# A log-sum-exp on one core: VectorE's program aligned to a block of 256 instruction slots

## The chip, the cores and the metric

The kernel runs on one core of a Trainium2 chip. A core has five engines that run their own instruction streams side by side: TensorE (PE in the profile), VectorE (DVE), ScalarE (ACT), GpSimd (POOL) and SyncE (SP), and DMA engines that move data between the device memory and the core's on-chip memory. [...] The metric is device time in microseconds; the median of three runs before the change is 162.67 us (162.56 to 162.72).

## The reference

The input x is 32 x 512 x 1024 floats; the result is the logarithm of the sum of exponentials over the last axis, 16,384 numbers.

```python
def reference(x, axis):
    x_max = np.max(x, axis=axis, keepdims=True)
    return (x_max.squeeze(axis) + np.log(np.sum(np.exp(x - x_max), axis=axis))).astype(np.float32)
```

The values of x are normal random numbers, 67.1 MB in all.

## The kernel before, in words

The 16,384 rows lie 128 to a partition: partition p holds rows 128p to 128p + 127, each 1,024 floats long. The kernel leaves out the subtraction of the maximum at first: it computes log(sum(exp(x))) directly, tests afterwards whether every sum lies between LOW and HIGH, and only if one does not, goes through all data again with the maximum subtracted (the fallback, lines 292 to 326).

The list CHUNKS cuts the 128 rows of a partition into 17 chunks of 16 rows down to 1. SP issues their loads in order into a ring of 51 row places (`load`, lines 129 to 149); a load into places that were used before first waits until the engine that read them last has signalled. For each chunk ACT takes the exponential in place (line 201) in one or two parts, and VectorE sums the rows of each part (line 221, or by halves with the fused add and reduce at line 208). Some rows of the smaller chunks are summed by ACT itself, with the accumulating output of its exponential (lines 191 and 228). ACT also takes the logarithms in three pieces (line 156), and SP stores the result (line 241).

The end is a test. VectorE takes the largest and the smallest sum (lines 256 and 257), compares with the bounds (line 246), TensorE adds up the votes over the partitions with two small matmuls (lines 267 and 270), and VectorE puts the count into one number, the verdict (line 275). SP, VectorE and ACT each load the verdict into a register (line 280) and branch on it: with a full count they jump over the fallback (the condition at line 292, whose branch the profile shows at line 328). SP then clears the semaphores (line 329), waits until the store has landed, and takes its count back (lines 330 and 331).

Nothing is reordered by a scheduler: each engine runs its instructions in the order in which the kernel writes them. The instructions of all engines stand in a first block, which ends with a barrier of the five engines, and in the body that follows; only the first load is moved ahead of that barrier (lines 335 to 343). The waits of an instruction are for the most part carried by the instruction itself.

VectorE's stream has 2 instructions in the first block, 55 in the body up to and with the branch, and 10 in the fallback with a branch at its end. Around the program stand instructions of the runtime that no line of the kernel names.

## Time and profile before

| what | value |
|---|---|
| median of three runs | 162.67 us (162.56 to 162.72) |
| the profiled execution's own time | 162.66 us |
| its span, first to last instruction of the kernel | 160.9 us |
| busy: DVE, ACT | 121.9 us (76%), 115.1 us (71%) |
| read from device memory | 67.11 MB, 417 GB/s over the span |
| share of the loads' packets in the time of 16 DMA engines | 97.3% |

The span runs from the first load that SP issues to the last instruction of the kernel's program. What the runtime does ahead of it and behind it is not in the span; the profiled execution's time is 1.7 us longer than the span. In the views, "<-" in brackets names what ended the idle time before an instruction, an engine's name with a q (DVEq) is its sequencer, and L221 is line 221. The chain of work that ended last is followed back from the last instruction to what released it. The trace holds more than the page prints: every update of a semaphore with its time, and the packets that fetch instructions for the engines' sequencers.

### The profile page before, as it was taken

Reading aid. Unit: us, or ns where it says so; the run is one execution under the profiler, and the core shown is the slowest. Engines: PE = TensorE matmul, PEld = TensorE weight load, DVE = VectorE, ACT = ScalarE, POOL = GpSimd, SP = SyncE. Lnnn points to the kernel's source line nnn. Section 1 sums busy time; section 2 is a strip of 40 time slices with the busy share of each in tenths; the row PEclk is TensorE's granted clock in tenths of the full one; section 3 lists DMA queues with packets and bytes.
Section 4 is the critical chain, followed back from the end, with each engine's and each line's share of the span. In section 5 each row is a group of like instructions: output and inputs, shape, how many; then the busy total and the mean of one; then the engine's idle time right before and its main releaser. Section 6 shows DMA issues by size and latency. Waiting matters only on the chain.

```text
span 160.9 us, 147 instructions
## 1 busy us (share of the span) xinstructions
PE 0.2 (0%) x2; PEld 0.1 (0%) x2; DVE 121.9 (76%) x51; ACT 115.1 (71%) x40; POOL 0.4 (0%) x8
## 2 busy tenths in 40 slices
PE   0000000000000000000000000000000000000000
PEld 0000000000000000000000000000000000000000
DVE  0028000004999999999999599999999999999894
ACT  3170006995089960999429993999199999999995
POOL 1000000000000000000000000000000000000000
DMA  7999799979989989989979999999999999999990
GB/s 269 497 489 489 321 412 521 440 342 521 424 358 521 424 358 521 424 358 521 424 326 456 456 456 440 424 424 424 413 412 412 474 420 403 433 428 425 402 405 31
DMA packets 2592, 67.18 MB, mean 417 GB/s; under 512 B 288, under 2 KB 416, under 8 KB 928
## 3 DMA queue, kind: packets, MB, share of 16 engines
q1 hardware_dynamic: 2592, 67.18, 97.3%
HBM read 67.11 MB, written 0.07 MB: 417 GB/s over the span
## 4 chain that ended last, share of the span: by engine, by line
DMA 49%; DVE 30%; ACT 20%; issue 0%; PE 0%
DMA ring<-in_x_dram 49%; DVE sums L221 29%; ACT ring L201 17%; ACT ring L228 3%; ACT ring L191 1%; ACT res L156 0%; DVE above L246 0%; PE votes L267 0%; DVE verdict L275 0%; PE votes L270 0%
## 5 line engine op out<-in xcount | busy, mean ns | idle before, releaser
L221 DVE TENSOR_REDUCE sums<-ring 128x8 f32<-128x8192 f32 (+5 forms) x14 | 111.2, 7994 | 36.8 <-ACT ring L201 36.8
L201 ACT ACTIVATE ring<-ring 128x8192 f32<-128x8192 f32 (+6 forms) x18 | 104.4, 5836 | 43.5 <-DMA ring<-in_x_dram 43.4
L208 DVE CUSTOM_DVE_ANT_0 ring<-ring 128x512 f32<-128x512 f32 x16 | 9.9, 688 | 0.0
L228 ACT ACTIVATE ring<-ring 128x1024 f32<-128x1024 f32 x8 | 8.2, 1042 | 0.0
L172 ACT ACT_TABLE_LOAD x1 | 1.3, 1283 | 0.8 <-PEq L360 0.8
L228 ACT ACTIVATION_READ_ACCUMULATOR ring<-ring 128x1 f32 x8 | 1.4, 176 | 0.0
L208 DVE DVE_READ_ACCUMULATOR2_ANT sums<- 128x1 f32 x16 | 1.3, 84 | 0.0
L191 ACT ACTIVATE ring<-ring 128x1024 f32<-128x1024 f32 x1 | 1.0, 1039 | 0.0
L246 DVE TENSOR_TENSOR above<-late,bounds 128x8 bf16<-128x8 f32 x1 | 0.2, 167 | 0.7 <-ACT res L156 0.7
L156 ACT ACTIVATE res<-sums 128x81 f32<-128x81 f32 (+1 forms) x2 | 0.5, 248 | 0.0
L275 DVE TENSOR_REDUCE verdict<-votes 1x1 int32<-1x6 f32 x1 | 0.2, 153 | 0.3 <-PE votes L270 0.3
L256 DVE TENSOR_REDUCE ends<-sums 128x1 f32<-128x124 f32 x1 | 0.3, 282 | 0.1
L267 PE MATMUL votes<-above,weights 128*1 128x6 bf16 x1 | 0.2, 166 | 159.6 <-DVE above L246 159.6
L257 DVE TENSOR_REDUCE ends<-sums 128x1 f32<-128x124 f32 x1 | 0.3, 270 | 0.0
L246 DVE TENSOR_TENSOR above<-ends,bounds 128x4 bf16<-128x4 f32 x1 | 0.2, 163 | 0.1
L156 ACT ACTIVATE res<-late 128x4 f32<-128x4 f32 x1 | 0.2, 173 | 0.0
L270 PE MATMUL votes<-above,weights 128*1 128x6 bf16 x1 | 0.2, 165 | 0.0
L267 PEld LDWEIGHTS votes<-above,weights 128*1 128x1 bf16 x1 | 0.1, 79 | 159.6 <-DVE above L246 159.6
L191 ACT ACTIVATION_READ_ACCUMULATOR ring<-ring 128x1 f32 x1 | 0.2, 155 | 0.0
L173 POOL MEMSET bounds<- 128x6 f32 x1 | 0.1, 104 | 0.4 <-POOLq L360 0.4
L174 POOL MEMSET bounds<- 128x6 f32 x1 | 0.1, 102 | 0.0
L176 POOL MEMSET weights<- 128x1 bf16 x1 | 0.1, 102 | 0.0
(6 smaller groups left out, 0.6 us busy)
## 6 DMA issues: line engine op xcount, KB each, us to landing
ring<-in_x_dram SPq DMA_DIRECT2D x1, 7680.0 KB, 24.7
ring<-in_x_dram SPq DMA_DIRECT2D x1, 7168.0 KB, 28.7
ring<-in_x_dram SPq DMA_DIRECT2D x1, 6656.0 KB, 35.8
ring<-in_x_dram SPq DMA_DIRECT2D x1, 4608.0 KB, 20.2
ring<-in_x_dram SPq DMA_DIRECT2D x2, 2048.0 KB, 16.0
ring<-in_x_dram SPq DMA_DIRECT2D x1, 3584.0 KB, 28.3
ring<-in_x_dram SPq DMA_DIRECT2D x1, 2560.0 KB, 27.3
ring<-in_x_dram SPq DMA_DIRECT2D x4, 512.0 KB, 27.0
```

What stands on the lines that cost most here:

```text
L156: nc.scalar.activation(out=res[:, lo:hi], in_=src, func=Ln, bias=bias).then_inc(act_done, 1)
L172: nc.scalar.preload_act_table_set("natural_log_exp_and_others")
L191: nc.scalar.activation(out=ring[:, s, lo:hi], in_=ring[:, s, lo:hi], func=Exp, accum_out=late[:, LATE - 1 + k : LATE + k],).then_inc(act_d ...
L201: nc.scalar.activation(out=ring[:, s + lo : s + hi], in_=ring[:, s + lo : s + hi], func=Exp).then_inc(act_done, 1)
L208: nc.vector.tensor_tensor_reduce(out=ring[:, s + j, : D // 2], in0=ring[:, s + j, : D // 2], in1=ring[:, s + j, D // 2 :], scale=1.0, scal ...
L221: nc.vector.reduce_sum(out=sums[:, row + lo : row + hi], in_=ring[:, s + lo : s + hi], axis=AX).then_inc(dve_done, 1)
L228: nc.scalar.activation(out=ring[:, s + j], in_=ring[:, s + j], func=Exp, accum_out=total(row + j),).then_inc(act_done, 1)
L246: nc.vector.tensor_tensor(out=above[:, :, lo:hi], in0=values.unsqueeze(1).to_broadcast([P, 2, hi - lo]), in1=bounds[:, :, lo:hi], op=Alu.i ...
L256: nc.vector.reduce_max(out=ends[:, :1], in_=sums[:, :late_row], axis=AX).then_inc(dve_done, 1)
L257: nc.vector.tensor_reduce(out=ends[:, 1:], in_=sums[:, :late_row], axis=AX, op=Alu.min).then_inc(dve_done, 1)
L267: nc.tensor.matmul(votes[:1, :K], lhsT=weights[:, :1], rhs=above[:, 0], start=True, stop=False)
L270: nc.tensor.matmul(votes[:1, :K], lhsT=weights[:, 1:], rhs=above[:, 1], start=False, stop=True).then_inc(counted, 1)
```

## The change

One statement is added ahead of the loop over the chunks. It is a directive on VectorE's stream to the loader: the next instruction of that engine is to stand at a slot number divisible by 256 (a slot holds one instruction of 64 bytes). The loader drops the directive and fills in as many slots as are missing. With `max_nops=0` none of the padding is executed: its first slot becomes a branch to the aligned instruction. The next instruction of VectorE is the first reduction (line 221, in the changed kernel line 224). The other engines' streams and the order of VectorE's instructions stay as they are; every line number behind the statement grows by three.

```diff
     nc.gpsimd.memset(weights[:, :1], 1.0)
     nc.gpsimd.memset(weights[:, 1:], -TOO_MANY).then_inc(pool_done, 1)
+
+
+    nc.vector.addr_align(256, max_nops=0)
 
     logged = 0
     done_before = [(0, 0)]
```

## The prediction

> **What bounds the kernel now.** I read the head of the page first, then the chain of work that ended last, then who waited for whom, then the start and the end of the timeline, and last the records that lie outside the span.

> ```profile
> span 160.9 us, 147 instructions
> ...
> PE 0.2 (0%) x2; PEld 0.1 (0%) x2; DVE 121.9 (76%) x51; ACT 115.1 (71%) x40; POOL 0.4 (0%) x8
> ...
> DMA 49%; DVE 30%; ACT 20%; issue 0%; PE 0%
> DMA ring<-in_x_dram 49%; DVE sums L221 29%; ACT ring L201 17%; ACT ring L228 3%; ACT ring L191 1%; ACT res L156 0%; DVE above L246 0%; PE votes L267 0%; DVE verdict L275 0%; PE votes L270 0%
> ```

> Half of the chain is the load of x, nearly all the rest is work on data that has landed, and "issue", time that nothing in the profile explains, is 0%. So inside the span no engine stands still for want of an instruction. The waits of VectorE (group, us in total, times, longest) say the same:

> ```profile
> DVE sums L221 <- ACT ring L201: 36.8, 4, 23.1
> DVE above L246 <- ACT res L156: 0.7, 1, 0.7
> DVE verdict L275 <- PE votes L270: 0.3, 1, 0.3
> ```

> All of its idle time is ended by another engine's data. The start of the timeline shows how early VectorE's program begins and how late it is needed:

> ```profile
> 0.88 0.10 POOL L176 MEMSET weights<- 128x1 bf16 x1
> 7.32 3.62 ACT L201 ACTIVATE ring<-ring 128x4096 f32<-128x4096 f32 x1 [5.26 <-DMA ring<-in_x_dram]
> 10.97 4.42 DVE L221 TENSOR_REDUCE sums<-ring 128x4 f32<-128x4096 f32 x1 [10.97 <-ACT ring L201]
> 25.50 13.00 ACT L201 ACTIVATE ring<-ring 128x15360 f32<-128x15360 f32 x1 [14.56 <-DMA ring<-in_x_dram]
> ```

> VectorE passes the opening barrier at 0.73 us (its semaphore wait runs from 0.711 for 0.021) and has nothing to do before 10.97. At the end, the branch over the fallback (L328) on the three engines that take it:

> ```profile
> L328 SPq COMPARE_BRANCH  x1: 45/45/45, 160.5 to 160.5; - x1
> L328 ACTq COMPARE_BRANCH  x1: 45/45/45, 160.5 to 160.5; - x1
> L328 DVEq COMPARE_BRANCH  x1: 67/67/67, 160.6 to 160.6; - x1
> ```

> The profiled execution took 162.66 us, its span is 160.94, so 1.72 us lie around the span; the median of the runs shown is 162.67, the same time. No view of the page reaches those 1.72 us, but the trace also holds semaphore updates and the packets of the instruction queue there. Times from the span's start, in us:

> ```
> last instruction: ACT branch ends 160.576, DVE branch ends 160.698, SP's last semaphore step ends 160.938
> semaphore 2, which no line of the kernel names: 159.954 | 160.775 160.814 161.351 161.374 | 161.472 161.510 161.544 161.591
> semaphore clears by block of numbers: 161.487 (207-255), 161.601 (156-206), 161.643 (54-104), 161.657 (105-155), 161.811 to 162.158 (7-53)
> semaphore 2 again: 162.422 162.456 162.494 162.539 162.562 | 162.659 162.698 162.732 162.779
> instruction queue: one packet of 8192 bytes at 161.819, 0.455 long
> ```

> Semaphore 2 steps five times up and four times back, a barrier of the five engines after the program. Where nobody is late, the up-steps are 34, 38, 45 and 23 ns apart (the second barrier). In the first one the fourth step is 0.537 us behind the third instead of 0.045, and all that follows waits for it. That is the place where the change can act.

> The first step (159.954) is TensorE's, the only engine then finished that had worked so late (its last result is signalled at 159.796, 0.158 before). Of ACT, SP and VectorE the first to end is ACT: 160.576, and the second step is 0.199 later. SP can't be at 160.775 or 160.814, it still runs its program. VectorE can hardly be, its branch has ended only 0.077 and 0.116 before. I take the fourth for VectorE and the fifth for SP, whose clears (the narrowest spacing, as in its own clear at L329) come first after the turn. Then VectorE needs 0.653 us from its branch to the barrier, ACT 0.199.

> **What could keep VectorE 0.45 us.** Its program is the longest: 2 instructions before the barrier's end, 55 up to the branch, 10 in the fallback and a closing branch; ACT has 44 in all, SP 38, PE and POOL 16 together. The only instruction packet near the end starts at 161.819, 1.12 us after VectorE's branch. The result's store shows the same lag: issued at 159.363, first packets about 160.21 to 160.53, landed after 1.5 us. So my reading is that VectorE's taken branch passes from one fetch block to the next, that this costs about 0.4 to 0.45 us, and that the packet is the refill which it triggers. It isn't a block fetched on demand: that would not have been there before 162.27 (161.819 + 0.455), and the fourth step comes at 161.351.

> **The change part by part.** One directive ahead of VectorE's first reduction. It removes no instruction, moves none between queues, and adds no wait and no DMA of the kernel; SP's and POOL's queues hold what they held.

> 1. Padding and its jump. VectorE executes one branch more at 0.73 us. The nearest row is L328 on DVE, 0.067 us. It lies in the idle time that ends at 10.97 with ACT's result (10.2 us of cover), so 0. If that cover were gone it would cost itself, 0.07.

> 2. Reaching the new block. It may need a fetch at 0.73 us, amid the loads. Lower bound 0 (the block is there). From the end of the trace a fetch takes 1.12 + 0.455 = 1.6 us in quiet queues. Among loads each packet of 61,440 bytes holds an engine for 2.3 us, so behind two of them it is about 1.6 + 4.6 = 6.2 us, landing at 6.9. The worst row is queueing behind everything, as the loads do (issue to landing, us):

> ```profile
> ring<-in_x_dram SPq DMA_DIRECT2D x1, 7168.0 KB, 28.7
> ring<-in_x_dram SPq DMA_DIRECT2D x1, 6656.0 KB, 35.8
> ...
> out_dram<-res SPq DMA_DIRECT2D x1, 64.0 KB, 1.5
> ```

> The first reduction takes 4.42 us and the second starts at 38.53, when ACT's second exp is done; so VectorE's start may slip to 34.1 us before anything later moves. Taken: 6.9 < 10.97, so 0. The bytes (16 KB at 417 GB/s) are 0.04 us of the loads, and I take 0 for them, too.

> 3. The crossing at the end goes. The 66 slots of body and fallback now start at slot 0 of a block of 256, and the code behind them has some 190 slots left. VectorE then would reach the barrier at 160.698 + 0.199 (ACT's row; with its slower branch, 67 to 45 ns, up to 0.30), so at 160.90 to 161.00 instead of 161.351.

> 4. What is late next: SP. It waits for the store's landing (last update 160.904) and ends at 160.938. From its last step to the barrier nothing is recorded; TensorE needed 0.158 and ACT 0.199 with a taken branch. By these, SP steps at 161.10 to 161.14 instead of 161.374, a gain of 0.24 to 0.28; if SP needs only 0.06, the gain is 0.37, and if it was as late as VectorE by itself, 0. I take 0.27, by the row that has no branch in it, as SP has none either, and some more haste of SP's sequencer (its semaphore waits last 17 ns, TensorE's 51). The rest of the tail hangs on this step and moves with it.

> Sum: 162.66 - 0.27 + 0 + 0 = 162.39 for the profiled execution, 162.40 against the median.

> [...]

> **The rivals.**

> A, the forecast: 162.40, by itself 162.28 to 162.52.

> B, nothing: the 0.45 us aren't the block's. VectorE's code behind the branch may be longer than ACT's, the fourth engine may be another, or SP may be the late one itself. For it: the fetch packet carries no engine's name, and VectorE is slower in the two rows next to it as well (its load of the verdict takes 545 ns, SP's 462). Against it: the packet's time. Time 162.67.

> C, more: the refill at 161.819 also holds the second barrier, whose first step (162.422) comes 0.148 after the packet's end at 162.274. Without it the step would follow the last clear (162.158) by TensorE's 0.158, at 162.316, 0.106 earlier; with A's 0.27 that is 0.38, 162.29. Against it: the block of clears that ends last isn't VectorE's by the order above.

> D, the other side: the jump at the end finds the code behind it not loaded. That takes the 1.6 us of item 2 from 160.698, and 0.2 to the barrier: 162.48 instead of 161.351, so 1.1 us more, 163.8. It decides only if the runtime's closing code has more than some 190 instructions, or if the aligned block's successor is never fetched ahead; one refill seen at the end speaks against both. A late fetch at the start would be its kin: past 34.1 us each us costs one, and with the 35.8 us row it would be 2.5, 165.1.

> **How the numbers follow.** A 0.59, B 0.21, C 0.08, D and its kin 0.12. A measurement of this kernel tells about 0.2%, 0.33 us, from no change, so the bound lies at 162.34. A's price is an estimate with about 0.07 us to either side, and some 18 of its 59 parts lie below that bound: faster 0.18 + 0.08 = 0.26; same 0.41 + 0.21 = 0.62; slower 0.12. The range takes in A, B and C with the spread of the runs (0.08 to each side): 162.22 to 162.78; D is left out.

> **What would show it.** Item 3 is right if the fourth step of semaphore 2 comes within about 0.3 us of VectorE's branch and the instruction packet at the end is gone; item 4 if SP's step comes 0.1 to 0.2 us after its last one; items 1 and 2 if an instruction packet shows in the first microseconds and the first reduction still starts at 10.97. Inside the span nothing should differ by more than 0.1 us. The prediction fails if VectorE is as late as before (B), or if the packet at the end stays while its step comes later (D).

## The result

The changed kernel takes 163.77 us (median of 6 runs, 163.68 to 163.83) against 162.66 us before (6 runs, 162.55 to 162.72): ratio 1.0070, 95% interval 1.0057 to 1.0083. It is 1.1 us slower, where the prediction said 162.40 and gave slower 0.12.

The profiled execution took 163.80 us. Its span is 162.435 us, 1.497 more than before; around the span lie 1.365 us, 0.357 less than before (1.722). So the end became cheaper, by somewhat more than the 0.27 forecast, and something inside the span, where the prediction saw nothing, cost four times as much. The head of the page and its list of DMA queues (packets, megabytes, share of 16 engines):

```profile
span 162.4 us, 148 instructions
...
q1 hardware_dynamic: 2592, 67.18, 96.4%
q14 instruction: 2, 0.02, 0.0%
```

Before, the list had q1 alone. Now two packets of the instruction queue fall inside the span. The chain that ended last, in order of time (start, us, what), of the kernel before:

```profile
0.78 24.69 DMA ring<-in_x_dram
...
25.50 13.01 ACT ring L201
...
38.53 16.16 DVE sums L221
...
54.71 28.93 DMA ring<-in_x_dram
...
122.02 24.68 DMA ring<-in_x_dram
```

and of the changed kernel:

```profile
0.78 26.25 DMA ring<-in_x_dram
...
27.05 13.01 ACT ring L204
...
40.09 16.16 DVE sums L224
...
56.27 28.83 DMA ring<-in_x_dram
...
123.48 24.72 DMA ring<-in_x_dram
```

The whole loss is in the first piece: 26.25 instead of 24.69, 1.56 us. Every later piece has its old length within 0.1 us and only starts later. Nor does VectorE wait for its own instructions; its three waits end as before, on other engines' data:

```profile
DVE sums L224 <- ACT ring L204: 38.2, 4, 24.1
DVE above L249 <- ACT res L156: 0.7, 1, 0.7
DVE verdict L278 <- PE votes L273: 0.3, 1, 0.3
```

The timeline shows both first loads late, and VectorE following them:

```profile
7.93 3.62 ACT L204 ACTIVATE ring<-ring 128x4096 f32<-128x4096 f32 x1 [5.88 <-DMA ring<-in_x_dram]
11.58 4.42 DVE L224 TENSOR_REDUCE sums<-ring 128x4 f32<-128x4096 f32 x1 [11.58 <-ACT ring L204]
27.05 13.00 ACT L204 ACTIVATE ring<-ring 128x15360 f32<-128x15360 f32 x1 [15.50 <-DMA ring<-in_x_dram]
```

ACT's first exponential starts 0.61 us later than before, its second 1.56. The reason stands in the records of single packets. The trace names no DMA engine, but in the first 26 us of the changed kernel's profile the packets sort into 16 rows by start and end, each packet starting within 0.012 us of the end of the one ahead of it. I take a row for an engine. Both instruction packets are in one row (start, us, length, bytes):

```
row with the instruction packets                 another row of the same profile
 4.172  0.611  16384                              4.589  0.611  16384
 4.779  0.309   8192  instruction                 5.197  0.611  16384
 5.085  1.147  16384                              5.804  0.611  16384
 ...                                              ...
 9.727  2.267  61440                              9.287  2.267  61440
11.991  0.321   8192  instruction                11.551  2.267  61440
12.300  2.929  61440                             13.814  2.267  61440
 ...                                              ...
ends the second load at 26.566                   the other 15 end it at 24.527 to 25.184
```

Each instruction packet takes 0.31 to 0.32 us itself, and the load packet behind it takes 0.54 and 0.66 us longer than its kind. That is 1.82 us on one engine of sixteen. Without them the row would have ended at about 24.75, among the others. The rest of the load waits for it: 26.566 against 25.174 for the latest row before. The load's semaphore shows the same without any sorting into rows. It takes 16 steps; fifteen are there by 25.551, the last comes at 27.031 (before: fifteen by 25.386, the last at 25.473), and ACT starts 0.02 us behind it. So 1.39 of the 1.56 us is the late row; the other 0.17 lies between the row's end and the last step (0.465, before 0.299), and no run shows why.

The end, by the same kind of records as in the prediction:

```
                                  before     changed
DVE's branch ends                160.698     162.195
fourth step of semaphore 2       161.351     162.440   (0.653, now 0.245 behind the branch)
SP's last step ends              160.938     162.435
fifth step                       161.374     162.570   (0.436, now 0.135 behind SP)
last clear to second barrier       0.264       0.264
instruction packet at the end    161.819        none
```

### The profile page after: what moved, and what is told of

It reads as the page before. It is cut to its first block, busy times and chain, and to the rows that moved or that the text cites. A ratio compares the mean times of both kernels' runs of the same rounds, so it can differ in the third digit from the quotient of the medians.

```text
span 162.4 us, 148 instructions
## 1 busy us (share of the span) xinstructions
PE 0.2 (0%) x2; PEld 0.1 (0%) x2; DVE 121.9 (75%) x51; ACT 115.1 (71%) x40; POOL 0.4 (0%) x8
## 4 chain that ended last, share of the span: by engine, by line
DMA 49%; DVE 29%; ACT 20%; issue 0%; PE 0%
DMA ring<-in_x_dram 49%; DVE sums L224 29%; ACT ring L204 17%; ACT ring L231 2%; ACT ring L194 1%; ACT res L156 0%; DVE above L249 0%; PE votes L270 0%; DVE verdict L278 0%; PE votes L273 0%
## 5 line engine op out<-in xcount | busy, mean ns | idle before, releaser
L156 ACT ACTIVATE res<-sums 128x81 f32<-128x81 f32 (+1 forms) x2 | 0.5, 250 | 0.0
L270 PE MATMUL votes<-above,weights 128*1 128x6 bf16 x1 | 0.2, 166 | 161.1 <-DVE above L249 161.1
L156 ACT ACTIVATE res<-late 128x4 f32<-128x4 f32 x1 | 0.2, 173 | 0.0
L270 PEld LDWEIGHTS votes<-above,weights 128*1 128x1 bf16 x1 | 0.1, 79 | 161.1 <-DVE above L249 161.1
## 6 DMA issues: line engine op xcount, KB each, us to landing
ring<-in_x_dram SPq DMA_DIRECT2D x1, 7168.0 KB, 28.6
ring<-in_x_dram SPq DMA_DIRECT2D x1, 6656.0 KB, 35.7
```

Of the source, the lines that this page charges most:

```text
L156: nc.scalar.activation(out=res[:, lo:hi], in_=src, func=Ln, bias=bias).then_inc(act_done, 1)
L270: nc.tensor.matmul(votes[:1, :K], lhsT=weights[:, :1], rhs=above[:, 0], start=True, stop=False)
```

## The experiments

The theory (T): two instruction packets among the loads make one DMA engine late, and a load lands with its slowest engine. The rivals: the loss belongs to VectorE or to aligned code as such, to the bytes, or to the first two loads alone. For the end, the theory C: VectorE's late step is the branch passing a block's end.

On the chips of these runs the kernel before spread wider than above (162.5 to 163.3 us), so each is read by its ratio to the runs of the kernel before beside it. Where one profile is set against the one profile of the kernel before, 0.1 to 0.2 us are of that spread: in the seven profiles whose first loads no instruction packet touches and no copy joins (late_align, mid_align, late128 and the four with empty instructions), the second exponential starts at 25.57 to 25.69, against 25.495 before. The diffs of mid_align, steal and the runs with empty instructions are against the kernel before, that of late128 against late_align, the others against the changed kernel.

**late_align: the directive ahead of the last compare instead.**

```diff
-    nc.vector.addr_align(256, max_nops=0)      # ahead of the loop over the chunks
...
     compare(0, 2, ends)
+    nc.vector.addr_align(256, max_nops=0)
     nc.vector.wait_ge(act_done, acts)
     compare(2, K, late[:, :n_late])
```

> The directive stands ahead of VectorE's last compare instead of ahead of its first reduction. Theory T (the two instruction packets of 8192 bytes rob one DMA engine in the middle of the loads, and a load lands with its slowest engine): the refill now comes after 158 us, when all loads have landed, so the span stays 160.9 (within 0.1), and the barrier after the program is freed of the crossing as in the changed kernel (the fifth step of semaphore 2 0.14 us behind SP's last step instead of 0.44): 162.36 (162.3 to 162.45). VectorE's jump lies in the 0.73 us in which it waits for ACT's last result. Rival L (aligned code as such, or the longer program, slows loads or engines, wherever the refill falls): span 162.4, time 163.8. Rival J (the jump costs VectorE more than its idle 0.73 us): the last compare starts later than 159.37 and the time lies between 162.5 and 163.5.

Measured: 164.61 us, ratio 1.0103 (1.0084 to 1.0122). VectorE's waits:

```profile
DVE sums L221 <- ACT ring L201: 37.0, 4, 23.1
DVE above L246 <- issue: 2.9, 1, 2.9
```

"issue": nothing in the profile ended this wait. The jump starts at 158.776 and the next instruction at 161.766, 2.99 us later, although ACT's result was there at about 159.6. The first instruction packet runs from 159.776 to 160.269, the second comes at 162.636, after VectorE has gone on. The loads were on time (second exponential at 25.613, before 25.495), so L falls and T holds for them. The forecast of the time missed: VectorE is late, as J says, and by more than J's range (to 163.5). What VectorE waited for no record names. That the code at the place the jump leads to was not there is my estimate, from the packet of 8192 bytes that runs within the wait; late128 below makes the jump shorter. The barrier was freed here too: its fourth step comes 0.245 behind VectorE's branch.

**pool_only: GpSimd aligned instead of VectorE.**

```diff
     nc.gpsimd.memset(weights[:, 1:], -TOO_MANY).then_inc(pool_done, 1)
+    nc.gpsimd.addr_align(256, max_nops=0)
-    nc.vector.addr_align(256, max_nops=0)
```

> VectorE's stream is as before; GpSimd, which has nothing to do after 0.98 us, is aligned behind its last memset instead. Theory T: GpSimd's refill robs a DMA engine in the same way: packets of the instruction queue in the first 15 us, first load 0.3 to 0.6 us later, second load 1.0 to 1.6 us later, end as before: 163.7 to 164.3. Rival V (the loss belongs to VectorE, its stream or its jump): no change, 162.66. No refill, if GpSimd's stream ends in the block that it jumps to and none is fetched: 162.66 as well, but then without instruction packets among the loads, which would decide nothing.

Measured: 163.74 us, ratio 1.0057 (1.0035 to 1.0080). Its packets, and the first piece of its chain:

```profile
q14 instruction: 2, 0.02, 0.0%
```

```profile
0.79 25.62 DMA ring<-in_x_dram
...
26.43 13.01 ACT ring L202
```

The packets come at 4.797 and 11.689, in one row that ends the second load at 25.945 against 25.326 for the latest of the others; the second exponential is 0.94 us late, a little under the 1.0 to 1.6 expected. VectorE's stream is unchanged, and the end is as late as before (0.651 from its branch to the fourth step). So the loss isn't VectorE's: rival V falls. The stretch behind the packets is smaller than for VectorE's, 0.22 and 0.35 us.

**both_start: VectorE and GpSimd aligned.**

```diff
+    nc.gpsimd.addr_align(256, max_nops=0)
...
     nc.vector.addr_align(256, max_nops=0)
```

> The changed kernel with GpSimd aligned as well. Theory T, where a load lands with its slowest DMA engine: if the two engines' refills go through different DMA engines, both are late side by side and the cost is the larger one: 163.6 to 164.0; if through the same, it adds up: 165.0 to 165.4. Rival S (what counts is the total of bytes or packets taken from the loads): adds up in either case, about 164.9 to 165.4, with the packets on two DMA engines.

Measured: 163.73 us, ratio 1.0054 (1.0035 to 1.0074). Four packets, in two rows, which end the second load at 25.97 and 26.73; the others end by 25.27. The load's semaphore has fourteen steps by 25.620 and the last two at 26.422 and 27.194. Twice the packets cost no more than VectorE's two alone (1.0070): here the slowest engine counts, not the sum. Rival S falls.

**mid_align: the directive ahead of the third chunk.**

```diff
     for i, (r, n_dve, parts, by_halves) in enumerate(CHUNKS):
+        if i == 2:
+            nc.vector.addr_align(256, max_nops=0)
```

> The directive stands ahead of VectorE's third chunk, so that the jump comes at about 38.6 us and the refill between 39 and 50 us, among packets of 65,536 bytes. Theory T: 16 DMA engines stay busy to the end, so what one engine loses there stays lost: the load that lands at 83.6 before comes 0.9 to 2 us late, and the end with it; with the barrier's 0.30 us back, 163.2 to 164.4. Rival F (only the first two loads are sensitive, later ones have slack): span 160.9, time 162.36.

Measured: 163.82 us, ratio 1.0063 (1.0044 to 1.0083). Packets at 44.070 and 49.747. In its chain the first load piece has its old length, the second is longer (28.93 before):

```profile
0.79 24.77 DMA ring<-in_x_dram
...
54.80 30.27 DMA ring<-in_x_dram
```

The loss, 1.34 us, moved with the packets. Rival F falls.

**slots_run: the padding executed.**

```diff
-    nc.vector.addr_align(256, max_nops=0)
+    nc.vector.addr_align(256, max_nops=255)
```

> The changed kernel, but the padding is executed as empty instructions instead of being jumped over, in VectorE's idle first 10 us. Theory T: what counts are the instruction packets among the loads. If straight-line code has its next block loaded ahead, one packet at most falls among the first loads instead of two: second load 0.4 to 1.0 us late, time 162.8 to 163.4 with the end's 0.30 back. If the two packets remain, 163.8 as with the jump.

**nops20: 20 empty instructions instead of a directive.**

```diff
+    for _ in range(20):
+        nc.vector.engine_nop()
```

> No directive. VectorE executes 20 empty instructions ahead of its first reduction, in its idle first 10 us, so all of its later code moves by 20 slots and is not jumped to. Theory T with crossing C (VectorE's late step in the barrier before the change is the branch at the end passing a block's end): the block's end now falls 10 to 20 instructions ahead of that branch, about 148 to 152 us, and is passed in straight line. No instruction packet among the first loads; one at about 149 to 153, when the chain of waits runs through ACT and no longer through the loads; span 160.9, the fifth step of semaphore 2 0.14 us behind SP's last step instead of 0.44, time 0.30 below before: ratio 0.998. Rival J (passing a block's end stalls VectorE for about 3 us in straight line too, as the jump did in the late run): a gap without a cause between two of the half sums, and since the last of them is due at 157.8, 0.5 to 2.5 us above before. Rival N (the late step is not the block's): the same as before, ratio 1.000.

Measured: 162.88 us, ratio 1.0008 (0.9997 to 1.0020): no gain. Yet the barrier is freed (fifth step 0.136 behind SP). The one packet comes at 147.681, the load packet behind it takes 1.12 us instead of 0.46, and the last load packet ends at 158.081 instead of 157.524. Neither J nor N: the loads still mattered there, which the expectation denied. Half of it was wrong: T holds longer than I thought.

**steal: two foreign packets of about the same size.**

```diff
+    for k in range(2):
+        nc.scalar.dma_start(out=scratch[k : k + 1],
+            in_=bass.AP(tensor=x.tensor, offset=x.offset, ap=[[2039, 1], [1, 2039]])).then_inc(extra, 16)
...
+    nc.sync.wait_ge(extra, 32)
     nc.sync.wait_ge(passed, 2)
```

> VectorE as before. ACT's queue copies 8156 bytes of x within device memory, twice, as one packet each, in its first 2 us; nothing reads the copy. Theory T (a foreign packet on one DMA engine makes that engine late, and the loads wait for it): packets of that size among the first load's, each followed by a longer load packet as in the changed kernel, the engine 0.7 to 1.8 us behind the others, the second load later by 0.5 to 1.5 us and the end by as much: 163.1 to 164.2. Rival I (the loss is peculiar to instruction fetches): no more than the bytes, 0.04 us: 162.7.

Measured: 163.08 us, ratio 1.0026 (1.0011 to 1.0040). The list of queues:

```profile
q1 hardware_dynamic: 2592, 67.18, 97.1%
q10 hardware_dynamic: 4, 0.02, 0.0%
```

The two packets of 8156 bytes stand at 4.830 and 6.355 in one row, 0.308 us each, and the load packets behind them have their usual 0.611. So the engine loses 0.62 us, not 0.7 to 1.8, and ends at 25.390, hardly behind the next (25.342); the second exponential starts at 25.766, at most 0.2 us behind that of the untouched runs above. Of the 0.36 us between the medians (163.08, before 162.72), 0.24 lie around the span (1.95 us, before 1.71), where no load is; the spans have medians of 161.1 and 161.0. So T's range of 0.5 to 1.5 us for the loads is missed, and the result is nearer to I: the bytes of two foreign packets cost the loads about 0.1 us. The stretch of the packet behind is, in these runs, peculiar to instruction packets, and it makes up 1.20 of the 1.82 us of the changed kernel's late row; why it comes is not shown.

**late128, start128: 128 slots instead of 256.**

```diff
-    nc.vector.addr_align(256, max_nops=0)
+    nc.vector.addr_align(128, max_nops=0)
```

> As the late run, with 128 slots in place of 256. From the run with executed padding: the gap of 0.46 us after the 61st of 189 empty instructions says that blocks are 128 slots long and that VectorE's first reduction stands at slot 67 of 256, so the last compare, 51 instructions on, stands at slot 118. Padding to 128 is 10 slots, into the block that follows. Theory T with crossing C: passing into the block that follows costs 0.41 us, here inside the 0.73 us in which VectorE waits for ACT; one refill packet about 159.5 to 160.5, after the loads; no 3 us gap; barrier freed: span 160.9, time 0.30 below before, ratio 0.998. Rival J2 (every jump to a block's first slot fetches it anew): last compare 2 to 2.4 us late as in the late run, 164.5.

> The changed kernel with 128 slots in place of 256: the padding is 61 slots and the jump leads into the block that follows. Theory T: one packet instead of two among the loads, at 2 to 9 us, 0.31 long and the load packet behind it 0.5 to 0.7 longer; the engine 0.85 to 1.0 late, the second load 0.4 to 0.9; with the end's 0.30 back 162.8 to 163.3. If the number of packets doesn't matter, or two come again, 163.8.

Measured for late128: 162.55 us, ratio 0.9984 (0.9971 to 0.9997), a little faster than before. The last compare starts when ACT's result is there (159.616, after a wait of 0.73 us as before), the crossing is hidden, one packet comes at 159.909. J2 falls: the 2.99 us of the late run came with the leap from slot 118 to 256, and the jump from 118 to 128 has none of them.

Measured for start128: 162.73 us, ratio 0.9998 (0.9987 to 1.0009), below the 162.8 to 163.3 expected and the same as before. One packet at 4.775; its row ends the second load at 25.600, and the second exponential starts at 26.095, 0.41 to 0.53 behind the untouched runs. The spans of all runs put the loss at 0.3 us (median 161.4, before 161.1), and about as much comes back around the span (1.34, before 1.71): the two cancel.

**nops10, nops14, nops15: where the refill falls.** The edit is that of nops20 with another count.

> 10 empty instructions ahead of VectorE's first reduction, no directive: the block's end falls just ahead of the last compare, in straight line. Theory T with crossing C: as with the directive of 128 slots at that place, crossing hidden in the wait for ACT, refill packet after the loads (158.5 to 160.5), not at 147.7 as with 20 empty instructions: time 0.25 to 0.30 below before, ratio 0.998. If the refill comes earlier than VectorE's place suggests, before 157, a load is late again and the ratio is 1.000 to 1.003.

Measured: 162.50 us, ratio 0.9982 (0.9969 to 0.9995), packet at 159.968. But SP's last step comes 1.87 us behind the store's issue, before 1.56 (in late128 1.71). The refill lies just ahead of the store's packets (from 160.311), and of the 16 steps of the store's semaphore one alone is late: fifteen by 161.014, the last at 161.314 (before 160.877 and 160.904). So here, too, one engine's share lands last.

> 14 empty instructions: the block's end falls just behind VectorE's bare semaphore wait ahead of the largest sum (157.83 in the kernel before), so the refill is asked for then and its packet should come at 159.0 to 159.5, between the last load (157.5) and the store's packets (160.2), instead of 159.9 to 160.0 as with 10, where the store landed 0.15 to 0.30 us later than without. VectorE's 0.41 us lie in its 0.73 us of slack. If so: store's issue to SP's last step 1.56 us as before, barrier freed, ratio 0.9970 to 0.9982. If the packet's place by the store is no cause, the ratio stays at 0.9982 or above.

Measured: 162.48 us, ratio 0.9978 (0.9964 to 0.9991), the lowest ratio, faster than both kernels; its interval overlaps those of nops10 and late128, so the time alone doesn't set it apart. Packet at 159.245, after the last load (157.73) and ahead of the store's packets (from 160.443); store to SP's last step 1.56, as without a refill. The crossing shows in VectorE's timeline:

```profile
157.94 0.08 DVE L210 DVE_READ_ACCUMULATOR2_ANT sums<- 128x1 f32 x1
...
158.56 0.28 DVE L258 TENSOR_REDUCE ends<-sums 128x1 f32<-128x124 f32 x1 [0.54 <-ACT res L156]
...
159.60 0.17 DVE L248 TENSOR_TENSOR above<-late,bounds 128x8 bf16<-128x8 f32 x1 [0.31 <-ACT res L156]
```

Its semaphore wait ends at 158.081 and the reduction starts at 158.556, 0.475 later instead of 0.050. The wait ahead of the last compare shrinks from 0.73 to 0.31: the slack paid. (The profile names ACT for the 0.54. It can't be: in the kernel before, the same reduction starts at 157.90, before that instruction of ACT ends at 158.13.)

> 15 empty instructions: the block's end falls one instruction earlier, just ahead of that semaphore wait. If the bare wait is what holds VectorE's sequencer back, the refill now comes early, among the last loads (as with 20, at 147.7), and the gain of the barrier is lost: packet before 157, ratio 0.999 to 1.002. If only the distance in instructions counts, it behaves like 14: packet at 159.0 to 159.5, ratio 0.997 to 0.998.

Measured: 162.90 us, ratio 1.0004 (0.9991 to 1.0017). One instruction fewer on the near side of the block's end, and the packet comes at 149.927, 9 us earlier. The gain is gone:

```profile
122.80 28.59 DMA ring<-in_x_dram
...
151.41 4.57 ACT ring L203 x2
```

Before, the chain had left the loads by 146.7; here a load ends a wait at 151.4. This is the first case of the expectation: at 149.9 VectorE still has a reduction ahead of it that waits for ACT until 154.2, and the packet comes 4.3 us before that all the same. In nops14, where the block's end lies behind the bare semaphore wait, it came 1.16 us after that wait had ended (158.081 to 159.245). So the two runs fit the expectation's first case; what in VectorE asks for the packet, and what holds it back, no run shows.

**The end in all runs.** What theory C says of the end can be read in every run (us; around the span is a run's time less its span, which is given to 0.1):

```
                                          branch to fourth step    around the span, all runs
VectorE's code unmoved: before, pool_only    0.651 to 0.653              1.64 to 1.76
VectorE's code moved: the other runs         0.245 to 0.253              1.32 to 1.46
VectorE's code unmoved: steal                0.659                       1.90 to 2.00
```

In every run that moves the block's end away from VectorE's branch the late step is gone. No run moves the code and leaves the block's end under the branch.

## Why the prediction was wrong

The step that failed is item 2, in its last sentence: the bytes of the new block were put at 16 KB by 417 GB/s, 0.04 us, and that at 0. It looked for the harm in the wrong place. All bounds of that item ask whether VectorE gets its instructions in time, and they were right: the first packet ended at 5.09 (estimate 6.9) and VectorE waited only for ACT. But the fetch also takes something from the loads, and dividing by the mean rate of 16 engines spreads it over all. It fell on one, with 1.82 us, of which the packets' own time is 0.63 and the stretch of the load packets behind them 1.20; and the page had said that the loads are the bound: DMA 49% of the chain, q1 97.3% of 16 engines. Measured, the term is 1.5 us (span 1.497 longer), and the first reduction starts at 11.58, not 10.97. The pool, both and mid runs show it without VectorE, without adding up, and elsewhere in time.

Behind it stands a second misreading: the block. The prediction took it for the directive's 256 slots, so it had the jump lead into the next one and left some 190 slots behind the code. No run shows a block of 256. The runs show an end at slot 128 (the gap of 0.461 us in slots_run); by the estimate of 128 slots the padding from slot 67 to 256 leads over the whole next block. Two packets came, where the padding to slot 128 cost one (start128, ratio 0.9998 against 1.0070).

Item 1 held: the branch is there, at 0.808, 0.051 us, hidden. Item 3 held: 0.245 us from VectorE's branch to the barrier, forecast 0.20 to 0.30, and the cause, the branch passing a block's end, rests on the gap between the empty instructions (0.414 us), on nearly the same at the forecast place in nops14 (0.475 instead of 0.050), and on the runs that move the end of the block. Item 4 held: SP is next, 0.135 behind its last step; the gain there is 0.30, forecast 0.27. Another 0.05 came at the turn of the barrier, from the fifth step up to the first step back (0.098 before, 0.044 now), which the forecast had left out. The order of the engines in the barrier, which was argued, is borne out for VectorE and SP: only these two steps moved.

Rival B falls with item 3. Rival C falls: without the packet at the end, the second barrier still starts 0.264 behind the last clear. Rival D had the time, 163.8, but not the mechanism: nothing was late at the end. Its kin, the late fetch at the start, was priced on VectorE's start past 34.1 us, so it missed the loads as well. The sentence "inside the span nothing should differ by more than 0.1 us" is the one that the profile refuted first.

Passing a block's end was hidden here where VectorE had slack: the wait of 0.73 us ahead of the last compare shrank to 0.31 in nops14 and stayed 0.73 in late128. At the end of the kernel before it cost 0.41 us in VectorE and 0.30 to 0.36 in the time.

## What to carry to other kernels

In this kernel, whose loads fill 97.3% of the time of 16 DMA engines, the changed stream's two instruction packets fell on one engine and cost it 1.82 us, where their own time is 0.63: price such a fetch by the lateness of that engine, not by the bytes over the mean rate. Find where a long stream passes a block's end (here slot 128, by the gap in slots_run), and shift the end with a few empty instructions to a place where the engine has slack and neither loads nor the store run; 14 of them gained 0.22% (0.09 to 0.36), where alignment at the start lost 0.70%. Look beyond the span, in semaphore updates and instruction packets, when the measured time is longer than the span.

## What the runs showed of the hardware that I had not expected

- A load packet right behind an instruction packet took longer in these runs: 0.53 to 0.66 us more behind VectorE's, whether the packet's usual time is 0.31 or 2.42 us (1.12 instead of 0.46 in nops20, 2.93 instead of 2.27 in the changed kernel), 0.22 and 0.35 more behind GpSimd's (pool_only), nothing behind an ordinary packet of 8156 bytes (steal, 0.611). Why is open.
- The jump from slot 118 to 256 cost VectorE 2.99 us with quiet load queues (late_align), of which 1.5 lie behind the end of the first packet (160.269 to 161.766). What happens in these 1.5 us no run shows.
- One instruction of shift, from behind the bare semaphore wait to ahead of it, moved the packet by 9.3 us (159.245 in nops14, 149.927 in nops15). Why that wait made the difference no run shows.
